# A transposed modulation matrix summed by VectorE's multiply-and-sum, 8192-byte activation buffers, an early norm and pairs in the first FFN

## The chip, the cores and the metric

The kernel runs on one core of a Trainium2 chip. The metric is the device time of one execution in microseconds (us), the median of three runs. Engines are named as in the profile: PE is TensorE (matmuls; PEld is its weight load), DVE is VectorE, ACT is ScalarE, POOL is GpSimd and SP is SyncE, which here does nothing but issue DMAs.

## The reference: what is computed

Two transformer blocks follow each other on x of 256 tokens by 2048 features, all in float32. The parts that matter here are the first block's:

```python
c_act = jax.nn.silu(c)
mod = c_act @ w_ada + b_ada                  # w_ada: 2048 x 12288
sh1, sc1, gt1, sh2, sc2, gt2 = jnp.split(mod, 6, axis=-1)
h = modulate(rms_norm(x, g_mix), sh1, sc1)   # h * (1 + scale) + shift
z = h @ w_in                                 # then two attentions, gates
merged = (jax.nn.sigmoid(gate_sb) * (o_sb @ w_o_sb)
          + jax.nn.sigmoid(gate_ds) * (o_ds @ w_o_dsa))
x = x + gt1 * (merged @ w_out)
h = modulate(rms_norm(x, g_ffn), sh2, sc2)
a = causal_dwconv(h @ w_gate, conv_w, conv_b)
y = (jax.nn.silu(a) * (h @ w_up)) @ w_down   # 5632 hidden features
x = x + gt2 * y
```

The second block has a norm, a mixer (one projection w_in_2, several attentions, w_out_2) and an FFN of the same sizes without modulation and convolution. The matrix w_ada is used once, for a single vector c: it is a matrix-vector product over 100.7 MB.

## The kernel before

**Tiling.** Features lie on the 128 partitions, in 16 tiles k, and tokens along the free axis, 256 of them. A product of a weight matrix with the activations goes block by block: 128 input features (k) by 128 output features (f). Float32 accuracy comes from splitting both operands into a high and a low half (type fp32r), and three products hi x hi, hi x lo and lo x hi.

**Weights.** Every weight piece is 128 x 1024, 512 KB, and is loaded by SP into one of 10 buffers (`rawp`, `rawx`). ACT copies it to its high half (`wh`, L296), DVE subtracts to get its low half (`wl`, L303), and PE uses both. `split_to` keeps these steps a fixed number of pieces ahead of PE.

**Matmul forms.** `mm_f` has two forms. Unpaired (L399 to L401) it makes three matmuls of 256 or 258 columns for one product: hi by the high half of the activations, hi by their low half, lo by their high half, all into one PSUM range. Paired (`pair=True`, L393 to L397) high and low half of the activations lie side by side, so one matmul of 512 columns serves hi, and one of 256 serves lo; the two halves of the PSUM tile are then added by the evacuation.

**Order.** The program is one list `items`, written out by hand: pieces of weights, pieces of w_ada ("ada") between them at chosen ratios (`RA`, `RL`, `MORE`), and calls. `run` walks through it. Smaller work (attention, norms, hand-overs) is done by Python generators that advance one step at each `tick`, that is after each 1.27 us of PE's columns. Each engine executes its instructions in the order in which they were emitted.

**Modulation.** w_ada is read as pieces of 128 input features by up to 512 output columns. In `split`, an accumulator `adaacc` of 128 x 512 per group of four output tiles collects w_ada[k] * silu(c)[k], one step per k: on DVE by one multiply-add (L330, first write L325), or, for a third to a half of the k, on ACT by a scaling (L327) and on POOL by an add (L328, first write L325). `ada_finish` adds the two accumulators on POOL (L366), waits some ticks, and then has PE sum over the partitions by multiplying with a column of ones (L370), one output tile after the other; L348 adds b_ada. The first two groups go partly through PE directly (L321, L355). `need_ada` runs ticks until a range of output tiles is there.

**First norm.** The squares of x are made on ACT (L594), added on DVE (L597, L598) and summed over partitions on PE (L601). `h_prep` makes the normalised and modulated input h, group of k by group of k.

**First FFN.** w_out's evacuation adds to x and, in `x_out`, writes x times gain as high and low half (L1158 is one of its forms) and its squares to `ssq`. The norm's factor `rb` is not applied to that input: gate and up are computed with the unnormalised input, and their evacuation multiplies by `rb`. The shift is carried by two extra columns of the activations, so that these matmuls have T + 2 = 258 columns, unpaired, and the activation buffers have 8 x 258 x 4 = 8256 bytes. `norm_gen` makes `rb` beside the first matmuls of the FFN. The projections and w_out_2 of the second block are unpaired too, with 256 columns; the second FFN and both w_down are paired.

**Stages in the profile** (us): start to 30.7; w_in in six groups of k with attention beside it to 408.2 (stage A); the gates, w_o_sb, w_o_dsa and w_out to 872.0 (stage B); the first FFN to 1634, of which 872 to 1050 still carries modulation (stage C); the mixer of the second block and w_out_2 to 2069.4; the second FFN to the end.

## Time and profile before

| | |
|---|---|
| median of three runs | 2815.79 us (2815.03 to 2815.88) |
| the profiled execution's own time | 2818.41 us |
| its span | 2816.6 us, granted clock 0.993 |
| PE, PEld | 2734.5 us (97%), 2496.7 us (89%) |
| DVE, ACT, POOL | 71%, 51%, 30% |
| DMA | 590 MB, 210 GB/s on average |
| chain that ended last | PE 76%, DVE 10%, DMA 5%, issue 4%, POOL 3%, ACT 2% |
| w_ada's pieces | 144 of 512 KB, 64 of 384 KB |

Busy time is the time in which an engine executes something. Matmuls are pipelined, so that PE's busy time contains waiting for weights and a lower clock too. [...] In a row of a group, "x85 | 125.2, 1474 | 10.9 <-ACT wh L296" means 85 instructions, 125.2 us in all, 1474 ns each on average, and 10.9 us of idle time just before them, most of it ended by ACT's L296.

## The change

The host hands over w_ada transposed, so that an output feature is a row. A piece is now 128 output features by 1024 input features, half of the sum for one output tile: 192 pieces of 512 KB, with 4 KB in a row. `cb` is silu(c), the same on all partitions: c is loaded to one partition, spread by four matmuls with a row of ones, and sent through Silu on ACT. Each piece takes one instruction on DVE, `tensor_tensor_reduce`: multiply by `cb`, sum along the row, start value b_ada or the first half's sum, result in a column of `mod`. ACT's scaling, POOL's adds, the accumulators, PE's column sums and `ada_finish` with its waits are gone; `need_ada` becomes an assertion. `cb`'s buffer is given back after stage A and B's first part, so c is kept in DRAM and loaded again, 1 MB to all partitions, on ACT's queue when w_out begins.

All activation buffers have 8192 bytes, and `mod`, the low halves of the weights and `gain` get pools of their own (other addresses).

The norm ahead of the first FFN is early: w_out's evacuation adds to x and makes squares (on POOL, from k = 12 on DVE); the generator `f_norm` then sums them on PE, makes `rb`, and for each k multiplies x by `rb` (POOL, the first two on DVE), applies gain and shift on ACT, and writes high half (ACT) and low half (DVE). `f_act` advances it two k ahead of the matmul that asks for one. With the shift in the input, gate and up of the first FFN have 256 columns and are paired, and so are the projections by features of mixer 2 and w_out_2; evacuations add the two halves (`gather`: ACT copies, DVE adds).

```diff
+    modp = ctx.enter_context(tc.tile_pool(name="modp", bufs=1))
+    mod = modp.tile([128, 96], F32, name="mod")
+    wq = ctx.enter_context(tc.tile_pool(name="wq", bufs=4))
+    gainp = ctx.enter_context(tc.tile_pool(name="gainp", bufs=1))
+    gain = gainp.tile([128, 48], F32, name="gain")[:, :16]
     ring = ctx.enter_context(tc.tile_pool(name="ring", bufs=13))
...
-    def slot(dt=F32, n=T):
-        return ring.tile([128, 8, n], dt, name="ring", tag="ring")
+    def slot(dt=F32):
+        return ring.tile([128, 8, T], dt, name="ring", tag="ring")
...
-        return [("ada", a, k, n) for k, n in pieces(NK, 128 * ADA[a][1])]
+        return [("ada", a, i, 1) for i in range(2 * ADA[a][1])]
...
+        if it[0] == "ada":
+            raw_of[idx] = r
+            c, half = ADA[it[1]][0] + it[2] // 2, it[2] % 2
+            nc.sync.dma_start(out=r, in_=t["w_adaT"][128 * c:128 * c + 128, RAW * half:RAW * half + RAW])
+            return
...
-        a = it[1]
-        first = a in (0, NKG)
-        if stage == 0 and k0 == 0:
...
-            elif own < (2 if first else 1):
...
-            elif side:
-                nc.scalar.activation(out=x, in_=x, func=AF.Copy, scale=cs)
-                nc.gpsimd.tensor_tensor(out=acc, in0=x, in1=acc, op=OP.add)
-            else:
-                nc.vector.scalar_tensor_tensor(out=acc, in0=x, scalar=cs, in1=acc, op0=OP.mult, op1=OP.add)
...
+        if stage == 0:
+            return
+
+        c, half = ADA[it[1]][0] + it[2] // 2, it[2] % 2
+        below = mod[:, c:c + 1] if half else V["b_ada"][:, c:c + 1]
+        nc.vector.tensor_tensor_reduce(out=r, in0=r, in1=P["cb"][:, RAW * half:RAW * half + RAW], scale=1.0,
+                                       scalar=below, op0=OP.mult, op1=OP.add, accum_out=mod[:, c:c + 1])
+        if half:
+            ada_done.add(c)
...
-        while not set(range(a, b)) <= ada_done:
-            tick()
...
-    def ada_finish(a):
...
+        assert set(range(a, b)) <= ada_done, (a, b, ada_done)
...
-    lut(out=cact, in_=V["c"], func=AF.Silu)
+    for u in range(4):
+        ps = psm()
+        nc.tensor.matmul(ps, ones[0:1, :], P["cb"][0:1, 512 * u:512 * u + 512], start=True, stop=True)
+        lut(out=P["cb"][:, 512 * u:512 * u + 512], in_=ps, func=AF.Silu)
+    cdram = dram.tile([1, D], F32, name="cdram")
+    nc.scalar.dma_start(out=cdram, in_=P["cb"][0:1, :])
...
-    a0, a1 = ada_items(NKG), ada_items(0)
+    a0 = ada_items(NKG) + ada_items(0)
     items.extend(a0[:2])
     call_item(first_norm)
-    items.extend(a0[2:] + a1)
+    items.extend(a0[2:-2])
+    call_item(lambda: h_scale(0))
+    items.extend(a0[-2:])
     call_item(first_h)
...
-                acts["f"] = Pair(n=T + 2)
+                acts["f"] = Pair()
...
+            if first:
+                P["cb"] = P["ft"].tile([128, D], F32, name="cb", bufs=1)
+                nc.scalar.dma_start(out=P["cb"], in_=bass.AP(tensor=cdram.tensor, offset=cdram.offset,
+                                                             ap=[[0, 128], [1, D]]))
...
+    def square(k):
+        yield
+        sq = ssq[0] if k == 0 else P["late"].tile([128, T], F32, name="sq", tag="sq")
+        nc.scalar.activation(out=sq, in_=xk(k), func=AF.Square)
+        if k >= 12:
+            nc.vector.tensor_add(out=ssq[0], in0=ssq[0], in1=sq)
+        elif k:
+            nc.gpsimd.tensor_tensor(out=ssq[0], in0=ssq[0], in1=sq, op=OP.add)
 
     def wout_evac(u):
         def evac(f, ps):
             k = 4 * u + f
             if k == 0:
                 ssq[0] = P["late"].tile([128, T], F32, name="ssq", tag="ssq")
-            x = xk(k)
-            add_scaled(x, ps, mod[:, 32 + k:33 + k])
-            pend(x_out(k, gain[:, k:k + 1], acts["f"], [(ssq[0], None)]))
+            add_scaled(xk(k), ps, mod[:, 32 + k:33 + k])
+            pend(square(k))
         return evac
+
+    def f_norm():
+
+        settle()
+        ps = psm()
+        nc.tensor.matmul(ps[:, :T], ones, ssq[0], start=True, stop=True)
+        rsqrt_of(rb, ps[:, :T], 1.0 / D, T)
+        for k in range(NK):
+            y = P["ft"].tile([128, T], F32, name="fy", tag="fy", bufs=4)
+            (nc.gpsimd if k > 1 else nc.vector).tensor_tensor(out=y, in0=xk(k), in1=rb, op=OP.mult)
+            nc.scalar.activation(out=y, in_=y, func=AF.Identity, scale=gain[:, k:k + 1], bias=mod[:, 48 + k:49 + k])
+            hi, lo = acts["f"](k)
+            nc.scalar.activation(out=hi, in_=y, func=AF.Copy)
+            nc.vector.tensor_sub(out=lo, in0=y, in1=hi.bitcast(F32))
+            yield k
+
+    f_done = [-1]
+
+    def f_act(k):
+        while f_done[0] < min(k + 2, NK - 1):
+            f_done[0] = next(gens["f"])
+        return act_of("f")(k)
...
     def wout_post():
-        drain([gens["shift"]])
-        gens["norm"] = start(norm_gen(list(late)))
-
-    def wout_pre():
-        open_ffn(1)()
-        gens["shift"] = start(shift())
+        assert set(range(48, 64)) <= ada_done
+        gens["f"] = f_norm()
 
     for u in range(4):
         add_group(Group("f", [(512, t["w_out"], 512 * u, idr)], 16, act_of("m"), wout_evac(u),
-                        pre=wout_pre if u == 0 else None, post=wout_post if u == 3 else None, pair=True),
+                        pre=open_ffn(1) if u == 0 else None, post=wout_post if u == 3 else None, pair=True),
...
-            bb = P["ft"].tile([128, 1], F32, name="bb", tag="bb", bufs=6)
             w = lambda j: V["conv_w"][:, NFF * j + ff:NFF * j + ff + 1]
             nc.gpsimd.memset(a[:, 0:2], 0.0)
-            nc.vector.tensor_copy(out=bb, in_=ps[:, T:T + 1])
-            nc.vector.tensor_mul(out=a[:, 2:], in0=ps[:, :T], in1=rb)
-            yield
-            nc.scalar.activation(out=a[:, 2:], in_=a[:, 2:], func=AF.Identity, bias=bb)
+            gather(a[:, 2:], ps)
+            yield
...
-    def ffn(names, act, n, gate, up, down, fill=None):
+    def ffn(names, act, gate, up, down, fill=None):
         wg, wu, wd = (t[x] for x in names)
         for half, (lo, hi) in enumerate(((0, NHALF), (NHALF, NFF))):
             for b in range(lo, hi, 4):
                 pre = settle if b in (0, NHALF) else None
-                add_group(Group("f", [(512, wg, 128 * b, idr)], 16, act, gate(b), n=n, pre=pre, pair=n == T), fill, RL[1])
-                add_group(Group("f", [(512, wu, 128 * b, idr)], 16, act, up(b), n=n, pair=n == T), fill, RL[1])
+                add_group(Group("f", [(512, wg, 128 * b, idr)], 16, act, gate(b), pre=pre, pair=True), fill, RL[1])
+                add_group(Group("f", [(512, wu, 128 * b, idr)], 16, act, up(b), pair=True), fill, RL[1])
...
-            nc.vector.tensor_mul(out=x, in0=ps[:, :T], in1=rb)
+            gather(x, ps)
+            nc.vector.tensor_mul(out=x, in0=x, in1=rb)
...
-    add_group(Group("f", [w2(KC, 512)], 16, act_of("z"), c_evac, pre=open_mixer, post=mixer_a_post))
+    add_group(Group("f", [w2(KC, 512)], 16, act_of("z"), c_evac, pre=open_mixer, post=mixer_a_post, pair=True))
...
-            add_to(x, ps, 1)
+            add_to(x, ps)
```

## Rows read from the trace of the kernel before

**Rows 1.** Stages: length, busy us (count) by engine, granted clock, DMA share, GB/s

```profile
0.00:30.70 30.70, 15.52 (x64) 14.72 (x64) 15.22 (x37) 9.82 (x13) 6.19 (x10) 1.00 1.00 326
30.70:408.20 377.50, 350.62 (x2439) 323.18 (x2440) 353.05 (x480) 216.28 (x397) 260.88 (x217) 0.98 0.79 252
408.20:872.00 463.80, 434.20 (x2687) 382.46 (x2686) 385.49 (x540) 248.95 (x371) 240.59 (x178) 0.97 0.80 256
872.00:1050.00 178.00, 175.86 (x1454) 174.73 (x1453) 162.78 (x206) 110.73 (x158) 83.83 (x66) 1.00 0.80 265
1291.10:1521.90 230.80, 230.80 (x1922) 230.77 (x1921) 146.50 (x219) 116.71 (x159) 20.24 (x34) 1.00 0.61 183
1521.90:1634.00 112.10, 112.10 (x642) 97.92 (x641) 76.51 (x88) 57.61 (x83) 27.72 (x26) 1.00 0.61 188
2069.40:2816.60 747.20, 743.67 (x4228) 648.04 (x4226) 436.60 (x511) 339.00 (x446) 112.21 (x91) 1.00 0.59 183
```

**Rows 2.** Groups by line on DVE, 30.7 to 408.2 (first row: one form): count, busy, mean ns

```profile
L303 DVE TENSOR_TENSOR wl<-raw,wh 128x1024 fp32r<-128x1024 f32 x85 | 125.2, 1474 | 10.9 <-ACT wh L296 10.9
L330 DVE SCALAR_TENSOR_TENSOR adaacc<-raw,cact,adaacc 128x384 f32<-128x384 f32 (+2 forms) x110 | 108.3, 984 | 1.6
L325 DVE TENSOR_SCALAR adaacc<-raw,cact 128x384 f32<-128x384 f32 (+2 forms) x12 | 7.5, 628 | 0.0
```

**Rows 3.** Groups by line on POOL, 30.7 to 408.2

```profile
L328 POOL TENSOR_TENSOR adaacc<-raw,adaacc 128x384 f32<-128x384 f32 (+2 forms) x50 | 61.3, 1226 | 19.5 <-ACT raw L327 14.2 <-issue 2.8 <-POOL ring L516 1.0
L325 POOL TENSOR_SCALAR adaacc<-raw,cact 128x384 f32<-128x384 f32 (+2 forms) x11 | 20.2, 1839 | 0.0
L366 POOL TENSOR_TENSOR adaacc<-adaacc 128x384 f32<-128x384 f32 (+2 forms) x11 | 17.7, 1605 | 21.0 <-DVE adaacc L330 21.0
```

**Rows 4.** Groups by line on DVE, 408.2 to 872

```profile
L303 DVE TENSOR_TENSOR wl<-raw,wh 128x1024 fp32r<-128x1024 f32 x130 | 191.8, 1486 | 57.9 <-ACT wh L296 57.7
L330 DVE SCALAR_TENSOR_TENSOR adaacc<-raw,cact,adaacc 128x512 f32<-128x512 f32 x74 | 82.9, 1121 | 0.9 <-DMA raw<-in_w_ada 0.9
L1158 DVE SCALAR_TENSOR_TENSOR ring<-ring,gain 128x256 fp32r<-128x256 f32 x13 | 10.4, 815 | 0.0
```

**Rows 5.** Groups by line on POOL, 408.2 to 872

```profile
L328 POOL TENSOR_TENSOR adaacc<-raw,adaacc 128x512 f32<-128x512 f32 x74 | 120.6, 1630 | 166.1 <-ACT raw L327 134.5 <-issue 20.6 <-DVE adaacc L330 7.5
L366 POOL TENSOR_TENSOR adaacc<-adaacc 128x512 f32<-128x512 f32 x11 | 18.4, 1676 | 14.8 <-DVE adaacc L330 14.8
```

**Rows 6.** Group by line on DVE, 1156.4 to 1291.1, POOL almost idle

```profile
L303 DVE TENSOR_TENSOR wl<-raw,wh 128x1024 fp32r<-128x1024 f32 x48 | 59.3, 1243 | 58.4 <-ACT wh L296 58.3
```

**Rows 7.** Groups by line on DVE, whole span: reductions and a multiply-add

```profile
L869 DVE CUSTOM_DVE_ANT_0 t<-pm,t 128x256 f32<-128x256 f32 x32 | 13.4, 418 | 0.8 <-POOL t L901 0.4 <-POOL t L1652 0.4
L869 DVE CUSTOM_DVE_ANT_0 t<-pm,t 128x128 f32<-128x128 f32 x32 | 9.0, 282 | 1.3 <-PE pm L891 0.4 <-POOL t L900 0.4 <-POOL t L1651 0.4
L869 DVE DVE_READ_ACCUMULATOR2_ANT st<- 128x1 f32 x64 | 5.2, 81 | 0.0
L1351 DVE SCALAR_TENSOR_TENSOR ring<-ring,vec,r 128x256 f32<-128x256 f32 x16 | 6.7, 479 | 0.0
```

**Rows 8.** Chain of waits: start us, us, one finish of four columns

```profile
768.93 1.26 PE pm L370 x8
```

**Rows 9.** Timeline of PE at the start: start us, us, instruction, idle before

```profile
13.98 3.78 PE L601 MATMUL pm<-ring,ones 128*128 128x256 f32 x8 [13.98 <-DVE ring L598]
30.72 0.58 PE L399 MATMUL pg<-ring,wh 128*128 128x256 f32 x1 [1.22 <-ACT ring L644]
```

**Rows 10.** Timeline of PE where w_out ends and the first FFN begins

```profile
872.01 0.29 PE L399 MATMUL pg<-ring,wh 128*128 128x258 f32 x1
```

**Rows 11.** Timeline of ACT: inverse root of the norm before the first FFN

```profile
879.66 1.28 ACT L197 ACT_TABLE_LOAD   x1
880.96 0.48 ACT L203 ACTIVATE r<-pm,epsc 128x256 f32<-128x256 f32 x1
```

**Rows 12.** Stages again: 4.2 us just behind a wait of PE

```profile
846.70:850.90 4.20, 4.18 (x16) 3.28 (x17) 4.09 (x9) 4.11 (x9) 1.27 (x2) 0.67 0.62 227
```

## What the change will do to the time

> **What bounds the kernel now.** I read the page first: over the whole span TensorE (PE) is busy 97%, VectorE (DVE) 71%, and DMA moves 210 GB/s on average. That says that PE is the bound nearly everywhere, and that a change elsewhere pays only in a stage where PE waits. So I cut the span into stages [rows 1]. The reader should compare the length of each stage with PE's busy time in it. In the first part of w_in (30.7 to 408.2, stage A) PE idles 26.9 of 377.5 us; from there to the end of w_out (stage B, to 872) 29.6 of 463.8; in 872 to 1050 (C) 2.1. In the gate and up part of the first FFN (1291.1 to 1521.9) PE never idles, and in the second FFN it idles 3.6 of 747.2. In A, DVE is busy 353.05 of 377.5 us, a share of 0.935: PE and DVE are both nearly full there, and each waits for the other. In B, DVE has a share of 0.83.

> PE's busy time also hides waste: a matmul that runs 0.96 of the clock or waits for its weights is busy. I therefore also counted columns: the program of stage A, at the pace of the undisturbed unpaired groups below, would fill PE for some 20 to 30 us less than the stage lasts.

> Then DVE by line. In A and B it does the subtraction that makes the low half of each weight (L303) and a multiply-add for modulation (L330) [rows 2, 4]. The reader should see that the same 128x1024 subtraction costs 1474 and 1486 ns there, and 1243 where POOL is nearly idle [rows 6]. In A, POOL is busy 0.69 of the time and in B 0.52 [rows 1], most of it with modulation's adds [rows 3, 5]. I read the difference of 0.23 to 0.24 us as DVE waiting while POOL works.

> **The change, part by part.** The sum is made against the profiled execution, 2818.4 us (span 2816.6). The median is 2815.8, so 2.6 is taken off at the end.

> *Price of one multiply-and-sum.* The kernel has the operation already, with one PSUM source: 418 ns at 256 columns, 282 at 128, and an 81 ns read of the accumulator behind each [rows 7]. The slope is 136/128 = 1.0625 ns a column, so 1024 columns take 418 + 768 x 1.0625 = 1234, plus 81: 1.315 us with POOL idle. With both sources in SBUF and three operands the nearest row is L1351, 479 ns for 256 columns, 61 more than the reduction: I take 1.35. No row has both sources in SBUF and an accumulator, so the other bound is a reduction at half the rate: 1234 + 1024 x 1.0625 + 81 = 2.40 us.

> *Startup: +1.5 (0 to +5).* Now the first norm's column sums start at 13.98 and the first weight matmul at 30.72 [rows 9]. The change puts four broadcast matmuls of 512 columns on PE and four Silus on ACT ahead of the squares on ACT. The four matmuls of 256 columns in L601 (recorded as eight passes) take 3.78 us, so the new ones take 7.6; the squares wait for the last Silu, and L601 comes about 3 us later. On DVE eight reductions (11 us) take the place of about as long a chain of small multiply-adds, column sums and their waits. Some of the 3 us is hidden by that, as h_scale(0) is now queued ahead of the last two.

> *Stage A: -28 (0 to -66).* Removed from DVE: 110 multiply-adds, 108.3 us, and 12 first writes (L325), 7.5 [rows 2]. Added: 68 reductions (two for each of the 28 columns of shift and scale of k 2 to 15, and the 12 items of MORE) at 1.51 us, 1.35 and half of the 0.23 to 0.3 that POOL's load adds, since POOL's share falls to about 0.43 when L325, L328 and L366 leave [rows 3]: 103. The subtractions fall with it by some 0.12 us each: -13. DVE's work becomes 353 - 116 + 103 - 13 = 327 us. I let the stage keep DVE's share of 0.935, so it lasts 350. Lower end: DVE had nothing to do with the end, 0. Upper end: PE at the clean pace, -45, and all of POOL's cover gone, -66.

> *Stage B: -20 (0 to -40).* Here 85 reductions at 1.44 (122) replace 74 multiply-adds (82.9 [rows 4]) and some 9 of first writes: +30. The subtractions go from 1486 to about 1308: 130 x 0.178 = -23. The subtraction for the unnormalised FFN input (L1158) leaves: -10. So DVE stays as full as it was. What goes is on PE and POOL: 11 finishes of four columns, 1.26 us of PE each [rows 8], 13.9; and chains over POOL (L328's 74 adds and 11 final adds [rows 5]), which DVE and PE's finishes wait for. 13.9 and a fifth of PE's idle 29.6 give -20.

> *Stage C: -2.* It has the same items, but only 2.1 us of idle time.

> *Early norm: +13 (9 to 20).* Today the first FFN starts at 872.01 with no idle time ahead [rows 10], because the norm's factor is multiplied in behind the matmuls; the inverse root runs from 879.66 to 881.4 with a table load [rows 11], beside PE. In the changed kernel PE needs the finished input. The chain behind the last w_out matmul: two multiply-adds 0.9, square 0.45, add 0.42, column sums 0.95, table load 1.28, Ln and Exp 0.48 each [rows 11], four small DVE operations of the correction 1.65, then multiply by rb, ACT's scale, ACT's copy and the low half, 1.8: 8.4 us, the small ones estimated by rows of 256 columns (L601's quarter [rows 9], L1351 [rows 7]). Onto it come one subtraction of weights queued ahead on DVE (1.24 [rows 6]), some 1.5 us for hand-overs, and 1.5 for PE's clock behind the gap: behind a wait that ended at 846.7 PE was granted 0.67 for 4.2 us [rows 12]. Behind the gap 15 more k come, most with one POOL operation (1.2 us by L328's 1.226 [rows 3]) and two of ACT, while the first group takes 4 x 0.35 = 1.4 us of PE per k; f_act keeps two ahead, so I put nothing on that, and up to 7 us if they don't keep up.

> *Pairs: -13.5 in the first FFN, -2 after it.* A gate/up half now holds 640 products of one 128x128 block (two of hi, one of lo): 230.8/640 = 360.6 ns, with 258 columns. The paired down half has 320 in 112.1, 350.3 ns, and the second FFN 2112 in 743.5, 352 ns [rows 1]. 1408 products at 351 instead of 360.6: -13.5. Most of that is the two columns fewer, not the pairing. Mixer 2 and w_out_2 have 768 products with 256 columns already; their evacuations get one ACT and one DVE operation more, hidden by a DVE with a share below 0.65 there: -2 (0 to -5.6).

> *Buffers of 8192 bytes: 0 (-14 to +14).* [...] The paired pace lies between 350 and 352 in the stages above, so half of that spread over 5500 products is 5, and I widen it.

> *Reload of c on ACT's queue: 0.* 1 MB at the stage's 256 GB/s [rows 1] takes 4.1 us, and the first four w_out pieces come ahead of the first reduction, 11 us of PE. If that cover is gone, up to 8.

> Sum: 1.5 - 28 - 20 - 2 + 13 - 13.5 - 2 = -51. 2818.4 - 51 - 2.6 = **2765**, with a range of its own of 2735 to 2798: the three large terms at half-way to their ends, in both directions.

> [...]

> **The rivals.** *Slower: the sum runs at half rate.* A reduction at 2.40 us instead of 1.35 adds 1.05 us to each of 68 in A, 85 in B, 31 in C and 8 at the start. A's DVE work becomes 327 + 71 = 398, over the 377.5 of today, at the share 0.935 426: +48. B's becomes 385 + 89 = 474 over 463.8: at a share of 0.95, +34. C gets 163 + 33 in 178: +17. Start: +9.5. With +13 for the norm and -15.5 for the pairs that is +106, so 2818.4 + 106 - 2.6 = **2922**. Divided by the 1.05 us that is a slope of about 150 us per us of price, from 2765 on; it turns slower above 1.35 + 51/150 = 1.69 us. Against it speak the rows of L1351 and L869. *Weak: only the parts on PE pay.* The waits of PE in A and B are ACT's high halves and DMA, not DVE (L303 waits for L296 57.7 us in B [rows 4]): A -10, B -5 instead of -28 and -20 (+33): **2798**. *Same: that, and the norm's gap is 20 to 25* because POOL's multiply and ACT's two passes per k come later than PE asks for them (+10), and half of what was left of A and B goes (+7): **2815**. *Fast: A and B run at PE's clean pace*, -55 and -35 instead of -28 and -20: **2723**. For it speaks that DVE and POOL are then short in no stage.

> **How the numbers follow.** Forecast 0.56, fast 0.11, weak 0.13, same 0.05, slower 0.15. The range 2715 to 2812 takes in the first three. Faster by over 0.2% (5.6 us, about what a measurement of this kernel can tell from no change) 0.80, within it 0.05, slower 0.15.

> **What would show it.** Right: reductions at 1.3 to 1.4 us where POOL is idle; subtractions in A below 1400 ns; A (first weight matmul to the first of k 7) near 350 us and B near 444; PE idle for 10 to 16 us ahead of the first FFN; its gate/up at 351 ns a product. Wrong: a reduction above 1.69 us; A no shorter although DVE's share falls (then ACT or DMA bounds it); a gap of over 20; a pace that moved in the second FFN, which the change leaves alone but for addresses.

## The result, and the profile after

The changed kernel takes 2764.46 us (median of 4, 2754.52 to 2771.06) against 2815.84: a ratio of 0.9816, interval 0.9801 to 0.983. 2765 had been forecast. Its profiled execution took 2759.37 us with a span of 2757.6, so 59 us of span went; that execution is one of the two shorter ones, which will matter below.

The stages of the trace after, in the columns of [rows 1]: start to end, length, busy time and count of PE, PEld, DVE, ACT and POOL, granted clock (a share of full speed), DMA share, GB/s. The cuts are at the same products of weights as there: start, A, B up to the last matmul of w_out, the gap ahead of the first FFN, the 62 products behind it, the rest of C, the second gate/up half, its down half, mixer 2 with w_out_2, second FFN:

```profile
0.00:34.97 34.97, 10.68 (x16) 4.98 (x16) 18.65 (x30) 11.57 (x16) 7.76 (x10) 0.84 0.89 330
34.97:394.40 359.43, 337.69 (x2375) 312.10 (x2376) 329.60 (x483) 194.48 (x347) 167.06 (x144) 0.98 0.80 260
394.40:822.70 428.30, 413.04 (x2599) 363.24 (x2597) 364.21 (x603) 196.34 (x284) 83.14 (x71) 0.99 0.84 279
822.70:834.50 11.80, 1.40 (x3) 0.53 (x3) 8.48 (x18) 5.36 (x9) 1.71 (x3) 0.65 0.51 164
834.50:866.10 31.60, 27.26 (x124) 21.94 (x125) 23.62 (x35) 22.11 (x41) 13.16 (x16) 0.86 0.54 166
866.10:1009.00 142.90, 142.79 (x824) 125.44 (x823) 124.27 (x172) 79.87 (x121) 15.46 (x24) 1.00 0.80 280
1244.30:1466.20 221.90, 221.90 (x1281) 195.27 (x1281) 142.37 (x180) 119.44 (x177) 21.28 (x34) 1.00 0.62 190
1466.20:1577.10 110.90, 110.90 (x641) 97.67 (x640) 75.91 (x87) 58.32 (x84) 28.95 (x27) 1.00 0.61 190
1577.10:2021.00 443.90, 432.15 (x2517) 363.88 (x2517) 319.38 (x609) 232.89 (x416) 77.41 (x65) 1.00 0.55 165
2021.00:2753.30 732.30, 732.30 (x4225) 644.45 (x4224) 437.07 (x511) 338.29 (x446) 110.94 (x91) 1.00 0.60 187
```

Against before: start 34.97 for 30.7 (+4.3); A 359.4 for 377.5 (-18.1); B 428.3 for 463.8 (-35.5); then a gap of 11.8 us with PE nearly idle, and 31.6 us for 62 products that took 24.1 before (+19.3 with the gap); the gate/up half 221.9 for 230.8 and the down half 110.9 for 112.1; mixer 2 and w_out_2 443.9 for 435.4 (+8.5); the second FFN 732.3 for 743.1 by the same products (-10.8). Mixer 2 and w_out_2 before, for the comparison:

```profile
1634.00:2069.40 435.40, 430.63 (x3285) 400.92 (x3284) 290.81 (x546) 222.57 (x384) 75.49 (x65) 1.00 0.56 169
```

DVE by line in A, as [rows 2]. Each sum is followed by a read of the accumulator, 79 ns:

```profile
L303 DVE TENSOR_TENSOR wl<-raw,wh 128x1024 fp32r<-128x1024 f32 x85 | 122.3, 1439 | 7.6 <-ACT wh L296 7.6
L311 DVE CUSTOM_DVE_ANT_0 raw<-raw,cb,mod 128x1024 f32<-128x1024 f32 x34 | 50.4, 1484 | 0.1
L311 DVE CUSTOM_DVE_ANT_0 raw<-raw,cb,vec 128x1024 f32<-128x1024 f32 x34 | 47.7, 1403 | 0.0
```

The mean price of a multiply-and-sum there is 1.444 + 0.079 = 1.52 us; 1.51 was forecast. DVE's work in A is 329.6 us; 327 was forecast.

DVE's timeline in the gap (start us, us):

```profile
822.66 0.42 DVE L1140 TENSOR_TENSOR ssq<-ssq,sq 128x256 f32<-128x256 f32 x1
823.00 1.00 DVE L1129 SCALAR_TENSOR_TENSOR ring<-pg,mod,ring 128x256 f32<-128x256 f32 x2
823.91 1.21 DVE L303 TENSOR_TENSOR wl<-raw,wh 128x1024 fp32r<-128x1024 f32 x1
825.04 1.28 DVE L311 CUSTOM_DVE_ANT_0 raw<-raw,cb,mod 128x1024 f32<-128x1024 f32 x1
826.25 0.08 DVE L311 DVE_READ_ACCUMULATOR2_ANT mod<- 128x1 f32 x1
826.25 1.22 DVE L303 TENSOR_TENSOR wl<-raw,wh 128x1024 fp32r<-128x1024 f32 x1
827.38 0.94 DVE L1140 TENSOR_TENSOR ssq<-ssq,sq 128x256 f32<-128x256 f32 x2
830.15 0.42 DVE L496 TENSOR_SCALAR mm<-pm 128x256 f32<-128x256 f32 x1 [1.82 <-ACT r L203]
```

The last two adds of squares (L1140), on which the norm waits, stand behind two subtractions of weights and one multiply-and-sum, 3.5 us.

## Experiments

Unless told otherwise, "changed" is the kernel after the change, and lengths of stages are read at the same products of weights. The paired pace is the time from the start of one paired product to that of the next. Code is cut to the lines that matter, with "..." where lines are left out.

**Modulation alone.** The kernel before, with the transposed w_ada, `cb`, the multiply-and-sum and the new order of the first pieces; `x_out`, `shift`, `norm_gen`, 258 columns and unpaired groups stay.

```diff
-        return [("ada", a, k, n) for k, n in pieces(NK, 128 * ADA[a][1])]
+        return [("ada", a, i, 1) for i in range(2 * ADA[a][1])]
...
+        nc.vector.tensor_tensor_reduce(out=r, in0=r, in1=P["cb"][:, RAW * half:RAW * half + RAW], scale=1.0,
+                                       scalar=below, op0=OP.mult, op1=OP.add, accum_out=mod[:, c:c + 1])
```

> The kernel before with the transposed modulation alone: DVE's multiply-and-sum, broadcast silu(c), no POOL adds and no column sums on PE; late norm, 258 columns unpaired and 8256-byte buffers stay. Theory (the sum of the prediction, sized by the trace after): start +4, stage A -18, stage B -31, C -2, so about -47 us against before, 2769 us. Rival (the gain before the first FFN comes from the new addresses and the lighter evacuation of w_out, not from modulation): -10 to -15 us, about 2803.

2765.5 us, all runs within 1 us. A and B, then mixer and second FFN:

```profile
35.00:393.70 358.70, 339.25 (x2374) 314.12 (x2375) 329.16 (x483) 194.74 (x347) 171.59 (x144) 0.99 0.80 261
393.70:824.90 431.20, 415.28 (x2600) 365.71 (x2599) 371.06 (x614) 201.45 (x297) 92.34 (x82) 0.99 0.83 277
1580.20:2015.80 435.60, 430.54 (x3286) 400.84 (x3285) 290.97 (x546) 222.53 (x384) 73.57 (x65) 1.00 0.55 169
2015.80:2758.90 743.10, 743.10 (x4227) 647.80 (x4226) 435.57 (x509) 339.17 (x446) 112.07 (x91) 1.00 0.59 184
```

Start +4.3, A -18.8, B -32.6, C -6.8, and from there on as before: this part alone gives as much as the whole change (2765.5 against 2764.5). The rest, that is early norm, pairs, 8192-byte buffers and pools, gives nothing in sum; the runs below show that gains and losses cancel in it.

**Each sum twice**, on modulation alone; the second goes to an unused column.

```diff
+        nc.vector.tensor_tensor_reduce(out=r, in0=r, in1=P["cb"][:, RAW * half:RAW * half + RAW], scale=1.0,
+                                       scalar=V["b_ada"][:, c:c + 1], op0=OP.mult, op1=OP.add, accum_out=dump)
```

> The kernel with the transposed modulation alone (2765.5 us), with each multiply-and-sum done a second time on DVE into an unused column, so that its price goes from about 1.43 to 2.86 us. Theory (DVE sets the length of the stages with modulation; the prediction's slope of 150 us per us of price): A +104, B +89, C +40, start +12, in all +215 to +245, so about 2990 us. Rival (DVE's work is mostly beside PE's, the gain came from what left PE and POOL): +60 to +100, about 2845.

2980.3 us, +214.8. A and B:

```profile
43.50:506.70 463.20, 377.51 (x2375) 344.83 (x2376) 421.92 (x619) 195.61 (x347) 170.27 (x144) 0.91 0.64 201
506.70:1012.30 505.60, 439.47 (x2599) 381.56 (x2598) 479.22 (x782) 201.60 (x296) 96.60 (x82) 0.95 0.74 236
```

A +104.5, B +74.4, C +26, start +8.5: DVE's work sets the length of A, where it rose by 92.8 us, and 150 us per us of price is the right slope. DVE's share of A is 0.911 here, 0.918 with single sums.

**About POOL's load of before**, on modulation alone: one add for each piece on a tile that no other engine uses.

```diff
         if stage == 0:
+            pa = P["pa"]
+            nc.gpsimd.tensor_tensor(out=pa[:, 1, :], in0=pa[:, 0, :], in1=pa[:, 1, :], op=OP.add)
             return
```

> The kernel with the transposed modulation alone (2765.5 us), with one 128x512 add on POOL for each modulation piece, on tiles of its own that nobody waits for: POOL's load of before without its chains. Theory (the subtractions and sums on DVE get longer beside POOL, and A and B feel it): subtractions from 1313 to about 1480 ns in B, DVE's busy time +8 us in A and +33 in B, the time +20 to +40, about 2795 us. Rival (POOL's load lengthens DVE's instructions, but not the path; or the longer subtractions had another cause): within 5 us of 2765.

2919.2 us, +153.7, nearly four times the upper figure. A and B, and DVE's groups in A, first with the adds, then with modulation alone:

```profile
36.90:467.10 430.20, 357.29 (x2375) 324.38 (x2376) 393.69 (x484) 195.92 (x347) 304.03 (x214) 0.95 0.69 217
467.10:956.70 489.60, 435.94 (x2600) 378.04 (x2599) 436.29 (x614) 201.63 (x297) 240.72 (x169) 0.96 0.76 244
```

```profile
L300 DVE TENSOR_TENSOR wl<-raw,wh 128x1024 fp32r<-128x1024 f32 x85 | 147.9, 1741 | 7.6 <-ACT wh L293 7.6
L310 DVE CUSTOM_DVE_ANT_0 raw<-raw,cb,vec 128x1024 f32<-128x1024 f32 x34 | 63.3, 1863 | 0.0
L310 DVE CUSTOM_DVE_ANT_0 raw<-raw,cb,mod 128x1024 f32<-128x1024 f32 x34 | 61.0, 1795 | 0.1
...
L465 DVE TENSOR_TENSOR ring<-pg,ring 128x256 f32<-128x256 f32 x36 | 14.1, 412 | 8.4 <-PE pg L348 8.4
```

```profile
L300 DVE TENSOR_TENSOR wl<-raw,wh 128x1024 fp32r<-128x1024 f32 x85 | 121.7, 1433 | 7.6 <-ACT wh L293 7.6
L308 DVE CUSTOM_DVE_ANT_0 raw<-raw,cb,mod 128x1024 f32<-128x1024 f32 x34 | 50.9, 1498 | 0.1
L308 DVE CUSTOM_DVE_ANT_0 raw<-raw,cb,vec 128x1024 f32<-128x1024 f32 x34 | 46.9, 1378 | 0.0
...
L463 DVE TENSOR_TENSOR ring<-pg,ring 128x256 f32<-128x256 f32 x36 | 14.0, 411 | 2.0 <-PE pg L346 2.0
```

The program of DVE is the same, yet its work in A grew by 64.5 us and the stage by 71.5; the subtraction went from 1433 to 1741 ns, the sum from 1.44 to 1.83 us. The add with one source in PSUM is as long as without POOL's adds (412 and 411 ns). No other engine waits for the adds, and PE's waits for DVE's low halves in A grew from 14.8 to 53.4 us, so the adds cost mostly through DVE (POOL's own later work stands behind them too). With one such add for each piece the kernel is slower than before. The 154 us is three times what the whole change gained, so it doesn't measure what leaving out the old adds was worth; it shows only that POOL's adds can cost through DVE.

**PE's column sums**, on modulation alone: one behind each finished tile, read by nobody.

```diff
+            ps = psm()
+            nc.tensor.matmul(ps[:, 0:1], P["cb"][:, 0:128], ones[:, 0:1], start=True, stop=True)
```

> The kernel with the transposed modulation alone (2765.5 us), with one column sum (128x128 by a column of ones) on PE behind each finished output tile, 96 in all, which nobody reads: PE's work of the old finish without its waits. Theory (a quarter of the 1.26 us that four columns took in the trace before, on PE's path where PE is nearly full): 0.31 us each, A +10, B +13, C +4, in all about +27, 2792 us. Rival (PE has idle time in A and B that takes them in, or a sum costs less where the next weights are loaded beside it): +10 or less.

2772.8 us, +7.3 (A -0.5, B +5.2): the rival. A and B:

```profile
34.90:393.10 358.20, 341.82 (x2441) 318.37 (x2442) 330.99 (x483) 195.16 (x347) 166.17 (x144) 1.00 0.80 261
393.10:829.50 436.40, 425.24 (x2685) 376.75 (x2683) 372.01 (x614) 201.82 (x297) 88.87 (x82) 0.99 0.83 274
```

A sum costs the path about 0.12 us in B (5.2 us for 43 of them), not 0.31.

**The norm's first step first.**

```diff
         gens["f"] = f_norm()
+        f_done[0] = next(gens["f"])
```

> The changed kernel with the first step of the early norm (last squares and adds, column sums, inverse root, first k) issued right behind w_out's last evacuation, ahead of the split of the next weight pieces. Theory (the gap of 12.1 us ahead of the first FFN holds 3.7 us of two weight subtractions and one multiply-and-sum on DVE and about 1 us of two weight copies on ACT that are queued ahead of the last squares and adds): the gap falls to 7 to 8.5 us, the time by 3 to 5 us. Rival (the weight pieces that are split later are then late themselves): the gap falls but PE waits the same time for the low halves of the first gate pieces, no change.

2764.4 us. From the end of w_out's last matmul to the start of the FFN's first the gap fell from 11.6 to 7.7 us, but PE then waited 4.6 us more at its second product:

```profile
833.69 0.76 PE L341 MATMUL pg<-ring,wh 128*128 128x512 f32 x1 [4.96 <-DVE ring L1165]
834.25 0.41 PE L342 MATMUL pg<-ring,wl 128*128 128x256 f32 x1
839.25 0.58 PE L344 MATMUL pg<-ring,wl 128*128 128x256 f32 x1 [4.58 <-ACT ring L1164]
```

The second k's multiply (L1161) stood behind two subtractions and a multiply-and-sum on DVE. From w_out's start to 62 products into the FFN it took 140 us instead of 138. So there was no gain, as the rival has it; but the wait was for the input's second k, not for the low halves of the weights that the rival names. Hence the next run:

**Three k first, and no modulation among the first pieces.**

```diff
+        for _ in range(3):
+            f_done[0] = next(gens["f"])
...
-                add_group(Group("f", [(512, wg, 128 * b, idr)], 16, act, gate(b), pre=pre, pair=True), fill, RL[1])
+                add_group(Group("f", [(512, wg, 128 * b, idr)], 16, act, gate(b), pre=pre, pair=True), fill, RL[1], 8 if fill and b == 0 else 0)
```

> The changed kernel with the first three k of the early norm issued right behind w_out's last evacuation (one k alone left the second k's multiply behind 3.7 us of weight work on DVE), and no modulation pieces among the first eight weight pieces of the first FFN. Theory (what the norm costs beyond its own chain is DVE's and ACT's queue order): the gap falls from 12.1 to about 8 us and the waits in the 62 products behind it from 10 to about 5 us; read over the stretch from w_out's start to 62 products into the FFN, 138.0 becomes about 129 us. Rival (the per-k chain over POOL, ACT twice and DVE is the limit itself): the waits move behind the gap and the stretch stays within 2 us of 138.

The same stretch took 130.7 us instead of 138.0: the theory, with two edits made at once and not told apart. The median stayed at 2763.6. In the profiled execution, 2763.56, the first FFN ran at 353.3 ns a product, and not at the 346.7 of the changed kernel's; its second gate/up half, to set beside the 221.90 above:

```profile
1243.00:1468.90 225.90, 225.90 (x1281) 194.99 (x1281) 142.40 (x180) 119.12 (x177) 21.80 (x34) 1.00 0.61 187
```

**Mixer 2 and w_out_2 unpaired.**

```diff
-            gather(x, ps)
-            nc.vector.tensor_mul(out=x, in0=x, in1=rb)
+            nc.vector.tensor_mul(out=x, in0=ps[:, :T], in1=rb)
```

and `pair=True` taken from those groups.

> The changed kernel with mixer 2's projections and w_out_2 unpaired again, their evacuations as in the kernel before. Theory (pairing costs the 8 us that the mixer lost in the trace after, by one ACT and one DVE operation more for each evacuation in chains of small operations): mixer and w_out_2 together 8 us shorter, about 2756. Rival (pairing itself gives 353 - 346.6 ns for each of 768 products there, and the loss is something else's): 5 us longer, about 2769.

2756.1 us (2747.4 to 2764.6); mixer and w_out_2, to set beside the 443.90 above:

```profile
1573.40:2011.50 438.10, 431.05 (x3286) 400.60 (x3285) 292.28 (x546) 222.58 (x384) 75.91 (x65) 1.00 0.56 168
```

5.8 us shorter; DVE has 27 us less to do there. PE's busy time is 431.1 for 432.2 and its idle time 7.0 for 11.7 us: the pairs saved nothing on PE, and their evacuations added waits.

**Buffers of 8256 bytes in the changed kernel.**

```diff
-        return ring.tile([128, 8, T], dt, name="ring", tag="ring")
+        r = ring.tile([128, 8 * T + 16], dt, name="ring", tag="ring")
+        return r[:, :8 * T].rearrange("p (a n) -> p a n", n=T)
```

> The changed kernel with activation buffers of 8256 bytes, of which 8192 are used; nothing else. Theory (the paired pace of 346.6 ns a product against 351 to 352 before comes from the buffers' addresses): the pace in the second FFN goes back to 350 to 352, and with some 5400 paired products the time rises by 20 to 27 us against the changed kernel, to about 2788. Rival (it comes from the separate pool of the low halves or from something else): the pace stays at 346.6 and the time at 2764 within the spread of 8 us.

2767.0 us, all runs within 2.3 us: between theory and rival. The second FFN took 736.4 us, 348.8 ns a product as a mean.

**The own pools, on modulation alone** (as the diff's first lines).

> The kernel with the transposed modulation alone (2765.5 us), with modulation, low halves and gain in the changed kernel's own pools; late norm, 258 columns and 8256-byte buffers stay. Theory (of the second FFN's 743.1 us in the trace, the pools account for the 6.7 that buffers of 8256 bytes with own pools left as a gain): second FFN 736.4 and time 2758, with runs within 1 us of each other. Rival (the pools do it only together with 8192 bytes or with pairs elsewhere): 2765.

2757.8 us (2757.0 to 2759.4), and 736.5 for the second FFN: the own pools give 6.6 of its 10.8 us, with late norm and without 8192 bytes. By the medians, modulation and pools are thus 6.7 us faster than the whole change, whose four runs lie on both sides (2754.5 to 2771.1): early norm, pairs and 8192-byte buffers, as built, bring nothing and seem to cost a little.

**The low halves back in the high ones' pool, in the changed kernel.**

```diff
-                hi, lo = half_of[idx, g, k0], view(wq.tile([128, 1024], F32R, name="wl", tag="wl"))
+                hi, lo = half_of[idx, g, k0], view(wp.tile([128, 1024], F32R, name="wl", tag="wl"))
```

> The changed kernel with the low halves of the weights in the same pool as the high ones again (their addresses now equal the high ones' modulo 2048 bytes); buffers of 8192 bytes stay. Theory (the pace of a paired product hangs on how the addresses of the low halves and of the activations lie): the two levels of 346.7 and 353.3 ns are replaced by others, with a mean of 350 to 353, and the time is 2765 to 2785. Rival (only the equal pitch of the buffers matters): both levels stay, 2754 to 2771 as the changed kernel itself.

2778.1 us, second FFN 743.8, 352 ns a product: 8192-byte buffers gain nothing without that pool. The second FFN in these three runs, in their order:

```profile
2023.10:2759.50 736.40, 736.40 (x4225) 647.25 (x4224) 436.55 (x511) 338.33 (x446) 111.39 (x91) 1.00 0.60 186
```

```profile
2015.30:2751.80 736.50, 736.50 (x4227) 647.29 (x4226) 436.06 (x509) 338.59 (x446) 112.13 (x91) 1.00 0.59 186
```

```profile
2031.70:2775.50 743.80, 743.80 (x4226) 648.81 (x4225) 436.84 (x511) 337.71 (x446) 111.72 (x91) 1.00 0.59 184
```

**Waits put into the FFN**: two one-column matmuls with a copy on DVE between, ahead of gate groups. They came into part of the first FFN too (7), 18 in all.

```diff
+            nc.tensor.matmul(ps[:, 0:1], ones, pause, start=True, stop=True)
+            nc.vector.tensor_copy(out=pause, in_=ps[:, 0:1])
...
-                pre = settle if b in (0, NHALF) else None
+                pre = (lambda b=b: stall(b)) if not fill else settle if b in (0, NHALF) else None
```

> The changed kernel with a short wait of PE on DVE (two one-column matmuls with a one-column copy between) ahead of each of the twelve gate groups of the second FFN. Theory (an undisturbed run of paired products keeps one of two paces, 346.7 or 353.3 ns, and takes it anew at a wait of PE): both paces occur among the twelve stretches, each held from one wait to the next; each wait costs 1 to 3 us, so 12 to 36 us and up to 14 of pace: 2775 to 2810. Rival (the pace is set once by the run or by the buffers): all twelve stretches at one pace.

2888.6 us, +124, or 6.9 for each wait, more than the 1 to 3 expected. PE's waits, then one wait (with PE's granted clock in the 5.1 us behind it), the stretch that follows, and the stretch behind the next wait:

```profile
PE pm L1262 <- DVE gain L1263: 69.0, 18, 5.8
```

```profile
1361.50:1366.40 4.90, 1.14 (x8) 1.01 (x6) 3.70 (x6) 2.98 (x6) 2.57 (x3) 0.81 0.22 47
1366.40:1371.50 5.10, 5.10 (x17) 4.39 (x17) 0.16 (x1) 0.00 (x0) 0.76 (x5) 0.51 0.53 196
1371.50:1413.50 42.00, 42.00 (x239) 36.27 (x238) 24.65 (x31) 21.21 (x31) 0.74 (x1) 1.00 0.58 173
1423.30:1463.80 40.50, 40.50 (x235) 35.65 (x234) 24.60 (x31) 20.70 (x31) 0.73 (x1) 1.00 0.60 177
```

A wait takes 3.8 us (69.0/18), in which PE waits for DVE. In the wait shown, the eight products behind it go at about 645 ns (5.2 us), at a granted clock of 0.51. From the start of one product to that of the next it is 353.3 ns in the first stretch and 346.7 in the second (by the rows, edges included, 42.00 x 2/239 = 351 and 40.50 x 2/235 = 345). Both paces occur, and each is held up to the next wait in this run: the theory.

**Both repairs**, three k first and the mixer unpaired, on the changed kernel.

> The changed kernel with both repairs: mixer 2 and w_out_2 unpaired, and the first three k of the early norm issued first, with no modulation pieces among the first eight weight pieces of the FFN. Theory (the two terms add): -5.8 and -7.3 us against the changed kernel at the same pace of the paired products, so 2746 to 2748 where both FFNs run at 346.7 ns a product, and 11 to 13 more where one of them runs at 353.3; the median near 2752. Rival (the two don't add, the mixer's share was chance): 2757 or more as the median.

2746.05 us (2740.2 to 2756.1, five runs), a ratio of 0.9758 (0.9737 to 0.978) to before: the fastest here, 18 us below the changed kernel and 6 below the 2752 expected. The stretch from w_out's start to 62 products into the FFN took 131.0, the mixer 437.7: 13.2 of the 18 are the two repairs, and the rest isn't accounted for.

## Why the prediction was right, and where only its sum was

*Price of the sum: right.* Where POOL is idle it takes 1.27 or 1.28 us and 0.08 for the read, as in the timeline above: 1.35 to 1.36, the value taken, 1.35. Half rate, 2.40, was a bound of the author's; no run shows it, and with it the slower rival is out: even beside POOL's load the mean in A was 1.52. L1351's row was rightly set against it: 479 ns are 61 more than the reduction's 418, not twice as long. The slope that had been worked out for this rival was right: doubling gave +214.8 for 1.43 us.

*Startup: +4.3 for +1.5*, inside its bounds. What was to hide the 3 us didn't.

*Stage A: -18.1 for -28.* DVE's work came as worked out (329.6 for 327). The step that failed is "I let the stage keep DVE's share of 0.935": the share became 0.917, and stayed near there when DVE's work was raised (0.911 and 0.915 with the sums twice and with POOL's adds). DVE's idle time in A rose from 24.5 to 29.8 us. By the profile its waits for ACT's copies out of PSUM (`pt`) grew from 5.0 to 10.2 us, and waits of 6.5 us came in `h_prep` (L610), while those for high halves fell from 11.2 to 7.8; why wasn't tested. For PE at its clean pace in A the prediction has three values (20 to 30, 45 and 55 us less) and no working, so its bound of -66 rests on nothing shown.

*Stage B: -35.5 for -20.* Modulation alone gives -32.6. The term was mis-sized in both pieces. PE's finishes were 13.9 of the 20; put back by themselves they cost 5. And "DVE stays as full as it was" was wrong: its work fell from 385.5 to 371.1 us with modulation alone, and the stage by over twice that. How much of the rest is the waits on POOL's chains wasn't separated. The rival "only the parts on PE pay" had it the wrong way round. The reload of c, put at 0, cost DVE a wait of 1.5 us here.

*POOL: the reading held, the size not.* That subtractions are longer because POOL works is shown by the POOL experiment. But their length doesn't go by POOL's share alone: 1474 ns in A before, at 0.69 [rows 1, 2], 1439 in A after, at 0.46, and 1741 at 0.71 in the POOL experiment. So the subtractions in A missed the sign "below 1400", though in B they came to 1313 for 1308. Why the same share costs so much more beside the multiply-and-sum is open.

*Early norm: +19.3 for +13.* The chain was right, its place in the queues not: one subtraction was counted ahead on DVE, and it was two and a multiply-and-sum, and behind the gap what had been put at "nothing", "up to 7 us", came to 7.5 us, 4.3 of it idle time of PE, with a granted clock of 0.86 over that stretch. Three k first, with no modulation beside them, took 7.3 off.

*Pairs and buffers: -31.8 for -13.5 in the profiled execution, and over a third of it chance.* From 62 products into the first FFN to its last gate/up product the change saved 19.8 us against modulation alone, in the last down half and the second FFN 12. The pace of 351 that had been put in lies near the mean, 350.0, of two: 346.7 and 353.3 ns. The profiled execution had 346.7 in both FFNs, 3.3 below the mean for some 4160 products, 13.7 us. The step that failed is that one pace was taken, and the buffers put at 0: moving buffers alone took the second FFN from 743.1 to 736.5 us (own pools), though a pace that moved there had been named as a sign of being wrong. That 13.7 is close to the bounds of 14 is luck: they came from widening half of the old spread, and the -31.8 lies 18.3 beyond the -13.5. Why moving buffers changes the pace isn't shown.

*Mixer: +8.5 for -2 (0 to -5.6): wrong in sign.* "Hidden by a DVE with a share below 0.65" was the failing step: the evacuations lie in chains of small operations, and PE's idle time there rose from 4.8 to 11.7 us though DVE's share is only 0.72 (and 0.67 before, not "below 0.65"); the wait for one small operation on DVE (L840) alone grew from 2.1 to 5.2. Without the pairs the stage is 5.8 us shorter; the other 2.7 wasn't separated.

*The sum.* A 10 short, norm 6, mixer 10 and start 3 against; B 15, C 5 and pace 18 in favour: the profiled execution lies 8 us below the forecast for it, and the median on it. 2765 was met because errors of 29 and 38 us cancel, which is luck. The range isn't what its words give either: half-way to the ends of A, B and the norm is 2734 to 2792, not 2735 to 2798. Of the parts as built, modulation pays, the own pools pay 7.7 us, and the rest together pays nothing.

## What to carry to other kernels

Ask of each engine that you unload whom its instructions were lengthening: here adds put back on POOL cost far more (+153.7 us), mostly through DVE, than column sums put back on PE (+7.3). A mean share is no cover (the mixer's idle time of PE grew by 6.9 us at a share of 0.72 on DVE): cost a wait by what stands ahead of it in its engine's queue, and issue the chain that PE waits for before the next pieces are split. And look at parts one at a time even when the total is as forecast: one of them gave as much as the whole, the others cancelled, and a kernel with the mixer's pairs undone and the norm issued earlier was 18 us faster still.

## What the runs showed of the hardware that was not expected

```profile
1255.40:1481.30 225.90, 225.90 (x1281) 195.03 (x1280) 142.27 (x180) 119.25 (x177) 21.60 (x34) 1.00 0.61 187
```

Over 1650 products of the first FFN that is 11 us, over 2111 of the second 14. That is about the distance between the upper and the lower pair of runs: the changed kernel's four lie at 2754.5, 2759.4, 2769.6 and 2771.1, those with the mixer unpaired at 2747.4 and 2750.0, 2762.3 and 2764.6. The kernel before has another pattern in the second FFN, the same in one group after the other: some 27 products at 353.3 ns, then 16 at about 349 (from 2077 us on, for one). The runs of the kernels with 8256-byte buffers and paired FFNs or modulation alone mostly stay within 1 to 2.5 us; with each sum twice the runs spread over 5.5, and those of the kernel before over 2 to 9. The two paces aren't the whole spread: the execution at 2759.4 already had 346.7 in both FFNs, and 2754.5 was seen too. Only one execution of each kernel was traced, and what decides between the two paces isn't shown.
